# Two declared orders in a two-layer decoder kernel: the second half of w_out behind the projection's last copies, the head outputs behind the gates' sixth product

## The chip, the core and the metric

The kernel runs on one core of a Trainium2 chip. The core has TensorE (PE, matrix products; "PEld" is its loading of weights), VectorE (DVE), ScalarE (ACT), GpSimd (POOL) and SyncE (SP, which here only starts transfers). Each engine works through its own list of instructions in order and waits, at the instruction whose turn it is, for semaphores of the others. The metric is the device time of one execution in microseconds (us).

## What is computed

Two layers of a decoder trunk on a sequence of 512 tokens with 1024 channels, all in float32. The part of a layer that the change touches is the end of the mixer:

```python
y_b = (jax.nn.silu(g_r) * y_r.reshape(B, S, RET_V_WIDTH)).astype(x.dtype)
merged = (jax.nn.sigmoid(gate_a) * jnp.einsum('bsc,cd->bsd', y_a, w_attn_proj)
          + jax.nn.sigmoid(gate_b) * jnp.einsum('bsc,cd->bsd', y_b, w_ret_proj))
return jnp.einsum('bsd,de->bse', merged, w_out)
```

`gate_a` and `gate_b` are columns of the input projection `x @ w_in + b_in`; `y_r` is the output of the four retention heads (2048 wide), `y_a` that of the attention (384 wide). Behind it come a residual with layer norm, a SwiGLU feed-forward part of width 2816, and a second layer norm.

## The kernel before, in words

Every float32 product is made of three faster ones. A value is split into a high part (a cast on ACT to the format that PE reads fast) and a low part (value minus high, on DVE), and PE adds high x high, high x low and low x high. The helper `hilo` (L106) does one split: one ACT instruction and one DVE instruction. Weights are loaded into buffers called `raw` (eight of 128 x 1024), split into `whi` and `wlo` (four each) and used. SP issues most loads in its own order; each waits until the buffer that it fills is free. POOL issues those that add to a buffer (L348, L1162), and also the transfers of the residual (L1349) and of the norm's parameters (L1360); the first step of the layer norm's root (L147) runs on POOL too.

Large products are cut into two by two blocks and computed with seven block products instead of eight (the Strassen-Winograd scheme). They are numbered 1 to 7 and run in the order 1, 2, 5, 3, 6, 7, 4 (`ORDER`). Some share an accumulator in PSUM (`CHAIN`): 1, 6, 7 and 4 add up in the two banks "A", 5 and 3 in "C". Between two products of one chain the sum so far has to be copied out (`sn`) before PE may go on adding to that bank.

The places that matter, in the order of the program in each layer:

- **The gates.** `gates(0)` and `gates(1)` (L1117) run such a scheme through `biased` (L501). Its `ev` is called behind each product for each half `a`: products 1, 5 and 6 are copied on ACT (L510, kept in the list `evicted`); product 2 is added in `left` (L1123); the result of product 3 is combined on DVE (L514) when product 6 is done; product 7 is subtracted on DVE (L517). The sigmoids of the right half are written to DRAM (`g_d`, L1132).
- **The head outputs.** During `gates(1)` the retention outputs are read back from DRAM (`y_d`) into `yr` (L1111). They are split into the left operand of the next product: `y_put` (L1113) writes quarters of `xh` and `xl`, and `s1` (L1164) forms one difference and splits it into `xs`. Three little instructions (L1145 to L1148) exist only to give this work a dependence on the gates: two casts write one or two columns of `xh` from a gate tile, and `one` is a scalar 1.0 computed from that tile, by which `s1` multiplies.
- **The attention weights** (`was`): eight small sums of nine matmuls, each multiplied into a gate tile `sg` on DVE (L1241).
- **The projection** with w_ret_proj, 28 weight units in the seven products, four units each. Unit n+2 is split while unit n is used (`emit`). Copies (`copies`, L1285), sums (L1327 to L1333) and gating (`gated`: L1268, L1269) follow the products, and the gated rows are transposed by PE (L1276) and split into `m`.
- **The output projection** with `m` and w_out: units 28 to 31 are the first half of w_out's columns, `stream[28:]`; the second half, `wo[4:]`, is split into the free `xs` by `tail_units` (L307). Results go to the residual `xtok` (L1379), the layer norm follows, and `xtok` is transposed (L205).

A scheduling framework sets the order of the instructions on each engine from dependences and its own estimate of times; where nothing binds two instructions, that estimate decides. `behind` (L83) declares an order of two instructions on one engine, without a semaphore. `seq` (L86) does so for a running chain per engine: while `chain` holds an entry for the engine, each instruction given to `seq` is put behind the one before it. The projection switches this on with `chain.update(act=None, dve=None)` and off with `chain.clear()`.

Of the kernel before, what the change touches and what calls it, by code (L numbers as in the profile page):

```python
# [12 lines left out]
F32 = mybir.dt.float32  # L13
# [3 lines left out]
ALU = mybir.AluOpType  # L17
# [3 lines left out]
P = 128  # L21
# [35 lines left out]
def hybrid_kernel(ctx, tc, x, rel_bias, w_in, b_in, w_attn_proj, w_ret_proj, w_out,  # L57
# [3 lines left out]
    pe, act, dve, pool = nc.tensor, nc.scalar, nc.vector, nc.gpsimd  # L61
# [4 lines left out]
    sm = ctx.enter_context(tc.tile_pool(name="sm", bufs=4, side="right"))  # L66
# [9 lines left out]
    xh = keep.tile([P, KD, S], F32R, name="xh")  # L76
    xl = keep.tile([P, KD, S], F32R, name="xl")
    xs = keep.tile([P, 4, 2, 4, 256], F32R, name="xs")
    dve.memset(mhalf, -0.5)

    evicted, chain = [], {}

    def behind(inst, other):  # L83
        tc.add_manual_dep(inst.ins, other.ins.name, ORDERED, reason="order on one engine")

    def seq(engine, inst):  # L86
        if engine in chain:
            if chain[engine] is not None:
                behind(inst, chain[engine])
            chain[engine] = inst  # L90
# [13 lines left out]
        return psm.tile([P, S], F32, tag="mm", name=name)  # L104

    def hilo(src, hi, lo):  # L106
        seq("act", act.copy(out=hi, in_=src))  # L107
        seq("dve", dve.tensor_tensor(out=lo, in0=src, in1=hi.bitcast(F32), op=ALU.subtract))  # L108

    def raw(name="raw"):  # L110
        return rawp.tile([P, 1024], F32, tag="raw", name=name)
# [1 line left out]
    def work(name):  # L113
        return wk.tile([P, S], F32, tag="w2", name=name)
# [194 lines left out]
    def tail_units(raws):  # L309

        out_ = []
        for j, r in enumerate(raws):
            v = xs[:, j].rearrange("p h k t -> p h (k t)").rearrange("p h (a b) -> p h a b", a=2)
            hilo(r, v[:, 0], v[:, 1])
            out_.append((v[:, 0], v[:, 1]))
        return out_
# [94 lines left out]
    def tall(right, n, left, ev, bias_=None):  # L411


        ps = {}
        for (i, an, bn), units in zip(ORDER, right.operands()):
            ks = [(u, k) for u in units for k in range(u[0].shape[1])]
            c = CHAIN[i]
            for a in range(2):
                fresh = i in FIRST
                if fresh:  # L420
                    ps[c, a] = psum("ps")[:, :n]
                if bias_ is not None and i in (1, 5):
                    o = (i != 1) * RV
                    mm(ps[c, a], pick[:, bias_:bias_ + 1].to_broadcast([P, P]), bh[:, o:o + n], True, False)
                    fresh = False
                ts_ = slice(a * P, (a + 1) * P)
                for j, ((h, l), k) in enumerate(ks):
                    p_ = ps[c, a]
                    ah, al = left(an, j, ts_)
                    mm(p_, ah, h[:, k], fresh and j == 0, False)  # L430
                    mm(p_, ah, l[:, k], False, False)
                    mm(p_, al, h[:, k], False, j == len(ks) - 1)
                    tick(STEP * n / 512)
                if i != 3:
                    ev(i, a, ps[c, a])
                if i == 6:
                    ev(3, a, ps["C", a])
            yield
# [63 lines left out]
    def biased(right, n, row, left, right_done):  # L502


        sn = {}

        def ev(i, a, ps):
            if i in (1, 5, 6):
                sn[i, a] = work("sn")[:, :n]
                evicted.append(act.copy(out=sn[i, a], in_=ps))  # L510
            elif i == 2:
                left(a, ps, sn[1, a])
            elif i == 3:
                dve.tensor_tensor(out=sn[6, a], in0=ps, in1=sn[6, a], op=ALU.subtract)  # L514
                right_done(a, sn[6, a])
            elif i == 7:
                dve.tensor_tensor(out=sn[5, a], in0=sn[5, a], in1=ps, op=ALU.subtract)  # L517
                right_done(2 + a, sn[5, a])
            elif i == 4:
                left(2 + a, ps, None)  # L520

        return tall(right, n, x_left, ev, row)
# [175 lines left out]
    def layer(ly, cp):  # L698
# [81 lines left out]
        with stage("attn") as ap_, stage("attw", 4) as aw:  # L780
# [62 lines left out]
            if ly == 0:  # L843
# [20 lines left out]
                for hf in range(2):  # L864
                    for i in range(2):
                        load_x(i, hf)
                    for g, j in tiles:
                        c = (C_QA, C_KA)[j] + g * GW
# [10 lines left out]
                late = []  # L879
# [95 lines left out]
            bias, tail = {}, []  # L975
            load_bias(0)
            for hp in range(HPG // 2):
# [21 lines left out]
                tail = t_  # L999
# [10 lines left out]
        with ret:  # L1010
# [81 lines left out]
            sga, ya, yb = [None] * NI, [], [[None, None], [None, None]]  # L1092
# [10 lines left out]
            def y_blocks():  # L1103
                yas.close()
                ret.close()
                sbp[0] = lay.enter_context(stage("sbp"))
                yr = yrs.enter_context(stage("yr", side="right"))
                for a, b in ((0, 0), (1, 0), (1, 1), (0, 1)):
                    yb[a][b] = [yr.tile([P, 4, 256], F32, tag=f"yr{a}{b}{u}", name="yr") for u in range(2)]
                    for u in range(2):  # L1110
                        nc.sync.dma_start(yb[a][b][u], y_part(a, b, u))  # L1111

            def y_put(o, u, r):  # L1113
                ks, ts_ = slice(4 * u, 4 * u + 4), slice(o, o + 256)
                hilo(r, xh[:, ks, ts_], xl[:, ks, ts_])

            def gates(c):  # L1117

# [19 lines left out]
            for n_, _ in enumerate(gates(1)):  # L1138
                if n_ == 0:
# [1 line left out]
                    for t in range(NG):  # L1141
                        ya_put(t)
                    y_blocks()
            late = sga[1][:, 1]
            act.copy(out=xh[:, 0:8:4, 0:1], in_=late[:, 0:2].unsqueeze(2))  # L1145
            act.copy(out=xh[:, 0, 256:257], in_=late[:, 0:1])
            one = sm.tile([P, 1], F32, tag="one", name="one", bufs=1)
            dve.tensor_scalar(one, late[:, 0:1], 0.0, 1.0, op0=ALU.mult, op1=ALU.add)  # L1148

            def block_w(b, u):  # L1150
                k = 8 * (b[1] == "2") + 2 * u
                c = (b[2] == "2") * S
                return wr_l[:, k:k + 2, c:c + S]
# [8 lines left out]
                pool.dma_start(r, block_w(b, u), accum_op=ALU.add)  # L1162

            def s1(u):  # L1164
                dve.scalar_tensor_tensor(out=a22[u], in0=a21[u], scalar=one, in1=a22[u], op0=ALU.mult, op1=ALU.subtract)
                hilo(a22[u], xs[:, u, 0], xs[:, u, 1])

            def s3_raw(u):
# [29 lines left out]
                o = 256 * (an[1] == "2" or an == "A12") + ts_.start  # L1198
                return xh[:, j, o:o + P], xl[:, j, o:o + P]

            for u in range(2):
                y_put(0, u, a11[u])
            for u in range(2):
                y_put(256, u, a12[u])
            for u in range(2):
                s1(u)
            more = [lambda f=f, u=u: f(u) for f in (s3_raw, s2_raw, s2_put, s4_raw, s4_put, s3_put) for u in range(2)]
# [2 lines left out]
            b22, wo, stream = [], [], []  # L1210

            def emit(n):
                g, u = divmod(n, 4)
                if g in (0, 2, 4, 6):
                    stream.append(unit(pch[u]))
                    if g in (0, 4):
                        add(pch[u], ("B12", "", "B21")[g // 2], u)
                elif g == 1:
                    stream.append(unit(b21[u]))
                    b22.append(load(block_w("B22", u), 2, S))  # L1220
                elif g in (3, 5):
                    stream.append(unit(b22[u]))
                    if g == 3:
                        seq("dve", dve.tensor_tensor(out=pch[u], in0=pch[u], in1=b22[u], op=ALU.add))
                        add(b22[u], "B12", u)
                else:
                    stream.append(unit(wo[u]))
                if g in (5, 6):
                    wo.append(load(wo_l[:, 2 * u:2 * u + 2, (g - 5) * S:(g - 4) * S], 2, S))

            for hf in range(2):
                for i in range(NI):
                    ps = psum("ps")
                    ks = [(u, k) for u in was[hf] for k in range(u[0].shape[1])]
# [53 lines left out]
            pss, sn = {}, {}  # L1288
            chain.update(act=None, dve=None)
            for n in range(28):  # L1290
                g, u = divmod(n, 4)
                i, an, _ = ORDER[g]
                c = CHAIN[i]
# [31 lines left out]
                for a in range(2):  # L1325
# [9 lines left out]
                    elif i == 4:  # L1335
                        if a == 0:
                            drain()
                        gated(2 + a, 0, pss[c][a], o_=work("sn"))
            chain.clear()
            emit(30)  # L1340
            emit(31)
        lay.close()

        fin = ExitStack()
# [40 lines left out]
        with stage("lp") as lp:  # L1385
            xc = [[lp.tile([P, 4, 256], F32, name=f"xc{a}{b}") for b in range(2)] for a in range(2)]
            ln_par(lp.tile([P, 2 * D], F32, name="lnp"), ln1_g[ly], ln1_b[ly])

            def m_tok(k, i):
                return (m[k // 4][:, e, k % 4, i * P:(i + 1) * P] for e in range(2))  # L1390

            def evo(hf, i, ps):
                residual(i, hf, ps, True, True)
                if hf == 1:
                    norm(i)
                    side.extend([nothing] * (6, 2, 5, 4)[i] + to_xT(xtok(i), i, xc))

            units = [stream[28:], tail_units(wo[4:])]
            for hf, toks in ((0, (0, 1)), (1, (0,)), (1, (1,)), (0, (2, 3)), (1, (2,)), (1, (3,))):
                while any(turns[i] for i in toks):  # L1400
                    side.popleft()()
                xstat(units[hf], S, m_tok, lambda i, ps, hf=hf: evo(hf, i, ps), toks=toks)
# [113 lines left out]
        for part, (f0, f1) in enumerate(FPARTS):  # L1516
# [31 lines left out]
            units = [[unit(r) for r in raws[0]], tail_units(raws[1])]  # L1548
# [67 lines left out]
```

## Time and profile before

| what | value |
| --- | --- |
| device time, median of 3 runs | 2111.55 us (2108.3 to 2112.28) |
| profiled execution, its time | 2108.74 us |
| its span in the trace | 2107.0 us |
| instructions | 33728 |
| busy: PE, weight loads, DVE, ACT, POOL | 99%, 88%, 79%, 54%, 13% |
| granted TensorE clock | 0.999 |
| moved by DMA | 366 MB, 174 GB/s over the span |

How to read the rows: an instruction row of the timeline has its start and its length in us from the span's start, the engine, the line of the kernel, the operation, "out<-in" by the program's names and the shapes, and in brackets how long the engine sat idle before it and what ended that. Ends of matmuls are modelled and overlap, so the step from one start to the next tells more than the length. A row of waits has the waiting engine, operand and line, what it waited for, and then the total in us, how many times, and the longest. "PE ps L96" are the matmuls of all products, since one helper records them.

### The profile page before, as it was taken

The page shows a single profiled execution, that of the slowest core. Times are in us where ns is not written, and L with a number is a line of the kernel's source. Part 1 is how long each engine was busy: PE and PEld are TensorE (multiplying, and loading weights), DVE is VectorE, ACT ScalarE, POOL GpSimd, SP SyncE. Part 2 cuts the span into 40 slices and gives each one's busy share as a digit, 9 for nine tenths or more (in the row PEclk, how much of TensorE's full clock was granted, in tenths as well). Part 3 has the DMA queues.
Part 4 walks back from the last instruction along what each step waited for, and adds up shares of the span by engine and source line. Part 5 has one row for each costly group of instructions (what it writes and reads, how often), then busy time and mean ns, then how long its engine had stood idle before and what let it go on. Part 6 is the DMA issues. An engine that isn't in the chain of part 4 may idle for free.

```text
span 2107.0 us, 33728 instructions
## 1 busy us (share of the span) xinstructions
PE 2079.4 (99%) x13130; PEld 1852.7 (88%) x13130; DVE 1656.0 (79%) x2359; ACT 1144.4 (54%) x1751; POOL 279.8 (13%) x280
## 2 busy tenths in 40 slices
PE   9999999999999999999999999999999999999998
PEld 8989888888787898999899898888887879989897
DVE  7666888786886698887787578897868877988876
ACT  5567654655654365555355766555655534655551
POOL 3111111101021101111030111111000211110101
PEclk9999999999999999999999999999999999999999
DMA  8866557666968358868258554657668782687771
GB/s 244 209 175 140 134 142 193 171 165 168 290 158 261 81 146 209 192 155 229 81 154 232 135 139 129 179 148 206 174 167 268 168 262 64 175 194 178 194 192 46
DMA packets 303297, 365.99 MB, mean 174 GB/s; under 512 B 22685, under 2 KB 214329, under 8 KB 303008
## 3 DMA queue, kind: packets, MB, share of 16 engines
q1 hardware_dynamic: 211904, 250.91, 37.6%
q0 software_dynamic: 63824, 100.11, 26.1%
q10 hardware_dynamic: 27408, 12.80, 2.2%
q8 instruction: 103, 1.69, 0.3%
q14 instruction: 58, 0.48, 0.1%
HBM read 342.11 MB, written 24.33 MB: 174 GB/s over the span
## 4 chain that ended last, share of the span: by engine, by line
PE 82%; DMA 6%; DVE 5%; issue 5%; ACT 1%; POOL 0%; POOLq 0%; DVEq 0%; SPq 0%; ACTq 0%
PE ps L96 73%; PE px L96 6%; DMA y_d<-yt 3%; DVE wlo L365 1%; DMA raw<-in_w_in 1%; PE px L596 1%; DMA yr<-y_d 1%; DVE wlo L108 1%; PE px L1058 1%; PE px L205 1%; DVE xs L108 1%; DMA raw<-in_w_out 1%; ACT whi L357 0%; DVE gb L1268 0%; POOL ry L147 0%
## 5 line engine op out<-in xcount | busy, mean ns | idle before, releaser
L365 DVE TENSOR_TENSOR wlo<-raw,whi 128x1024 fp32r<-128x1024 f32 (+1 forms) x518 | 602.3, 1172 | 175.9 <-ACT whi L357 162.1
L357 ACT CAST whi<-raw 128x1024 fp32r<-128x1024 f32 (+1 forms) x518 | 516.1, 1008 | 388.9 <-PE ps L96 145.0
L96 PE MATMUL ps<-xs,whi 128*128 128x256 f32 x2176 | 399.5, 284 | 0.4 <-ACT sn L828 0.4
L96 PE MATMUL ps<-whi,xs 128*128 128x512 f32 (+1 forms) x1152 | 349.2, 373 | 3.4 <-ACT sn L510 2.3
L96 PEld LDWEIGHTS ps<-xs,whi 128*128 128x128 f32 x2176 | 339.4, 192 | 4.9 <-issue 1.7
L96 PE MATMUL ps<-xh,whi 128*128 128x256 f32 (+1 forms) x1104 | 318.3, 290 | 1.7 <-ACT xh L107 1.4
L96 PE MATMUL ps<-xl,whi 128*128 128x256 f32 (+1 forms) x1104 | 315.5, 286 | 0.0
L96 PE MATMUL ps<-xh,wlo 128*128 128x256 f32 (+1 forms) x1104 | 315.0, 286 | 0.0
L96 PE MATMUL ps<-xs,wlo 128*128 128x256 f32 x1088 | 308.0, 283 | 1.2 <-DVE wlo L365 1.2
L96 PEld LDWEIGHTS ps<-whi,xs 128*128 128x128 f32 x1152 | 210.0, 188 | 40.0 <-ACT sn L510 4.0
L96 PEld LDWEIGHTS ps<-xh,whi 128*128 128x128 f32 x1104 | 210.3, 191 | 9.7 <-ACT xh L107 2.8
L96 PEld LDWEIGHTS ps<-xl,whi 128*128 128x128 f32 x1104 | 211.4, 191 | 3.0 <-DVE xl L108 0.6
L96 PE MATMUL ps<-wlo,xs 128*128 128x512 f32 (+1 forms) x576 | 213.2, 370 | 0.8 <-DVE wlo L365 0.8
L96 PEld LDWEIGHTS ps<-xh,wlo 128*128 128x128 f32 x1104 | 211.2, 191 | 1.5
L96 PEld LDWEIGHTS ps<-xs,wlo 128*128 128x128 f32 x1088 | 208.5, 192 | 1.8 <-DVE wlo L365 1.8
L96 PE MATMUL ps<-whi,xh 128*128 128x512 f32 (+1 forms) x512 | 193.7, 378 | 7.7 <-ACT sn L1285 5.3
L348 POOL DMA_DIRECT2D raw<-in_w_in x80 | 97.2, 1224 | 712.6 <-DMA raw<-in_w_in 235.5
L96 PE MATMUL ps<-wlo,xh 128*128 128x512 f32 (+1 forms) x512 | 190.8, 373 | 0.0
L96 PE MATMUL ps<-whi,xl 128*128 128x512 f32 (+1 forms) x512 | 190.2, 372 | 0.0
L381 DVE TENSOR_TENSOR raw<-raw 128x1024 f32<-128x1024 f32 (+1 forms) x148 | 171.8, 1168 | 0.8
L96 PE MATMUL ps<-whi,ht 128*128 128x512 f32 x544 | 170.1, 391 | 0.0
L107 ACT CAST whi<-raw 128x1024 fp32r<-128x1024 f32 (+1 forms) x102 | 100.6, 1001 | 97.3 <-PE ps L96 78.6
(247 smaller groups left out, 3272.8 us busy)
## 6 DMA issues: line engine op xcount, KB each, us to landing
raw<-in_w_in SPq DMA_DIRECT2D x168, 512.0 KB, 5.1
raw<-in_w_in POOLq DMA_DIRECT2D x64, 512.0 KB, 8.4
raw<-in_w_ffn_up SPq DMA_DIRECT2D x64, 512.0 KB, 4.6
raw<-in_w_ffn_down SPq DMA_DIRECT2D x52, 512.0 KB, 4.8
raw<-in_w_ffn_gate SPq DMA_DIRECT2D x44, 512.0 KB, 5.2
raw<-in_w_ffn_gate POOLq DMA_DIRECT2D x40, 512.0 KB, 7.1
raw<-in_w_in SPq DMA_DIRECT2D x56, 256.0 KB, 4.7
raw<-in_w_ret_proj SPq DMA_DIRECT2D x24, 512.0 KB, 4.4
```

Source lines behind the costliest of these rows:

```text
L96: pe.matmul(ps, lhsT=a, rhs=b, start=start, stop=stop, skip_group_check=True)
L107: seq("act", act.copy(out=hi, in_=src))
L108: seq("dve", dve.tensor_tensor(out=lo, in0=src, in1=hi.bitcast(F32), op=ALU.subtract))
L205: pe.transpose(px[:, d * P:(d + 1) * P], src[:, (4 * hf + d) * P:(4 * hf + d + 1) * P], ident)
L348: pool.dma_start(r, self.src({"P1": "B12", "P3": "B22"}[n], u), accum_op=ALU.add)
L357: c = act.copy(out=h, in_=src)
L365: dve.tensor_tensor(out=l, in0=src, in1=h.bitcast(F32), op=ALU.subtract)
L381: dve.tensor_tensor(out=r, in0=r, in1=self.t["B22" if n == "P2" else "B21", u], op=ALU.add)
L596: pe.transpose(px[:, hh, j * P:(j + 1) * P], ss[od][:, hh, j * P:(j + 1) * P], ident)
L1058: pe.transpose(px[:, t * P:(t + 1) * P], ys[i][:, t * P:(t + 1) * P], ident)
```

## The change

It does three things, all of them to orders.

First, `ev` keeps the DVE instruction that combines product 3 (in the new list `combined`). The head outputs' work no longer has its artificial dependence: the two casts, the scalar `one` and the multiplication by it are removed. Instead each of the four `y_put` casts is declared to stand behind the last copy of the gates (`evicted[-1]`), and each `s1` behind the last combination (`combined[-1]`); `s1` is a plain subtraction.

Second, `tail_units(wo[4:])` is called before `chain.clear()` and not after it, so its four splits stand in the chain behind everything that went through `seq` before: on ACT behind the last casts of weight units 30 and 31, on DVE behind the last gating and those units' low parts.

Third, `hilo` and `y_put` return their two instructions, so that they can be named.

```diff
-    evicted, chain = [], {}
+    evicted, combined, chain = [], [], {}
...
     def hilo(src, hi, lo):
-        seq("act", act.copy(out=hi, in_=src))
-        seq("dve", dve.tensor_tensor(out=lo, in0=src, in1=hi.bitcast(F32), op=ALU.subtract))
+        c = act.copy(out=hi, in_=src)
+        d = dve.tensor_tensor(out=lo, in0=src, in1=hi.bitcast(F32), op=ALU.subtract)
+        seq("act", c)
+        seq("dve", d)
+        return c, d
...
             elif i == 3:
-                dve.tensor_tensor(out=sn[6, a], in0=ps, in1=sn[6, a], op=ALU.subtract)
+                combined.append(dve.tensor_tensor(out=sn[6, a], in0=ps, in1=sn[6, a], op=ALU.subtract))
                 right_done(a, sn[6, a])
...
             def y_put(o, u, r):
                 ks, ts_ = slice(4 * u, 4 * u + 4), slice(o, o + 256)
-                hilo(r, xh[:, ks, ts_], xl[:, ks, ts_])
+                return hilo(r, xh[:, ks, ts_], xl[:, ks, ts_])
...
-            late = sga[1][:, 1]
-            act.copy(out=xh[:, 0:8:4, 0:1], in_=late[:, 0:2].unsqueeze(2))
-            act.copy(out=xh[:, 0, 256:257], in_=late[:, 0:1])
-            one = sm.tile([P, 1], F32, tag="one", name="one", bufs=1)
-            dve.tensor_scalar(one, late[:, 0:1], 0.0, 1.0, op0=ALU.mult, op1=ALU.add)
-
...
             def s1(u):
-                dve.scalar_tensor_tensor(out=a22[u], in0=a21[u], scalar=one, in1=a22[u], op0=ALU.mult, op1=ALU.subtract)
+                behind(dve.tensor_tensor(out=a22[u], in0=a21[u], in1=a22[u], op=ALU.subtract), combined[-1])
                 hilo(a22[u], xs[:, u, 0], xs[:, u, 1])
...
-            for u in range(2):
-                y_put(0, u, a11[u])
-            for u in range(2):
-                y_put(256, u, a12[u])
+            for o, r in ((0, a11), (256, a12)):
+                for u in range(2):
+                    behind(y_put(o, u, r[u])[0], evicted[-1])
...
-            chain.clear()
             emit(30)
             emit(31)
+            tail = tail_units(wo[4:])
+            chain.clear()
         lay.close()
...
-            units = [stream[28:], tail_units(wo[4:])]
+            units = [stream[28:], tail]
```

What the order of the instructions becomes, in layer 0 (layer 1 is the same). New lines are three higher than old ones up to L1146 and three or four lower behind.

ACT in `gates(1)`, from the last sigmoid of product 2 on, before. `xh<-yr` are head casts, `sn<-ps` the copies of product 5, `whi` casts of the gates' weights:

```order
L1126 ACTIVATE sg_5386<-sn_5716 128x512
L1145 CAST xh_79<-sg_5386 128x2
L1146 CAST xh_79<-sg_5386 128x1
L107 CAST xh_79<-yr_5735 128x4x256
L107 CAST xh_79<-yr_5736 128x4x256
L510 COPY sn_5811<-ps_5797 128x512
L510 COPY sn_5827<-ps_5813 128x512
L357 CAST whi_5833<-raw_5656 128x1024
```

and now:

```order
L1129 ACTIVATE sg_5386<-sn_5716 128x512
L513 COPY sn_5811<-ps_5797 128x512
L513 COPY sn_5827<-ps_5813 128x512
L360 CAST whi_5833<-raw_5656 128x1024
L360 CAST whi_5836<-raw_5659 128x1024
L360 CAST whi_5865<-raw_5662 128x1024
L360 CAST whi_5868<-raw_5665 128x1024
L513 COPY sn_5883<-ps_5686 128x512
```

The head casts have left the place between the gate and the copies of product 5; the first of them now stands behind both copies of product 6 and the two weight casts that follow.

DVE in `gates(1)` before, from the first head difference to the second subtraction of product 7 (`sn<-ps,sn` are L514, `sn<-sn,ps` L517):

```order
L1165 SCALAR_TENSOR_TENSOR yr_5743<-yr_5739,one_5979,yr_5743 128x1024
L365 TENSOR_TENSOR wlo_5834<-raw_5656,whi_5833 128x1024
L365 TENSOR_TENSOR wlo_5837<-raw_5659,whi_5836 128x1024
L381 TENSOR_TENSOR raw_5656<-raw_5656,raw_5652 128x1024
L381 TENSOR_TENSOR raw_5659<-raw_5659,raw_5654 128x1024
L365 TENSOR_TENSOR wlo_5866<-raw_5662,whi_5865 128x1024
L365 TENSOR_TENSOR wlo_5869<-raw_5665,whi_5868 128x1024
L108 TENSOR_TENSOR xl_80<-yr_5747,xh_79 128x4x256
L514 TENSOR_TENSOR sn_5883<-ps_5797,sn_5883 128x512
L108 TENSOR_TENSOR xs_81<-yr_5743,xs_81 128x1024
L1165 SCALAR_TENSOR_TENSOR yr_5744<-yr_5740,one_5979,yr_5744 128x1024
L514 TENSOR_TENSOR sn_5901<-ps_5813,sn_5901 128x512
```

and now, from the second weight operation behind the same point on:

```order
L368 TENSOR_TENSOR wlo_5869<-raw_5665,whi_5868 128x1024
L517 TENSOR_TENSOR sn_5883<-ps_5797,sn_5883 128x512
L517 TENSOR_TENSOR sn_5901<-ps_5813,sn_5901 128x512
L1162 TENSOR_TENSOR yr_5743<-yr_5739,yr_5743 128x1024
L368 TENSOR_TENSOR wlo_5912<-raw_5656,whi_5911 128x1024
L520 TENSOR_TENSOR sn_5811<-sn_5811,ps_5686 128x512
L368 TENSOR_TENSOR wlo_5915<-raw_5659,whi_5914 128x1024
L108 TENSOR_TENSOR xl_80<-yr_5735,xh_79 128x4x256
L520 TENSOR_TENSOR sn_5827<-sn_5827,ps_5702 128x512
```

The two differences and the head operations have moved from in front of the two combinations to behind them.

ACT at the end of the projection before, from the cast of weight unit 25 on (`m1<-px` follow PE's transposes, `sn<-ps` are the copies of product 7, `xs<-raw` the second half of w_out):

```order
L107 CAST whi_6636<-raw_6007 128x1024
L107 CAST xs_81<-raw_6615 128x1024
L107 CAST m1_6409<-px_6654 128x4x128
L1285 COPY sn_6661<-ps_6142 128x512
L1285 COPY sn_6662<-ps_6143 128x512
L107 CAST whi_6671<-raw_6009 128x1024
L107 CAST whi_6689<-raw_6011 128x1024
L107 CAST xs_81<-raw_6640 128x1024
```

and now:

```order
L107 CAST whi_6632<-raw_6003 128x1024
L107 CAST m1_6405<-px_6650 128x4x128
L1281 COPY sn_6657<-ps_6138 128x512
L1281 COPY sn_6658<-ps_6139 128x512
L107 CAST whi_6667<-raw_6005 128x1024
L107 CAST whi_6685<-raw_6007 128x1024
L107 CAST whi_6703<-raw_6525 128x1024
```

The four `xs` casts, and their four low parts on DVE, now follow the split of unit 31. On PE the transposes of the gated rows in product 4 (L1276, now L1272) stand five and sixteen matmuls later than before, and in layer 0 the first transposes of `xtok` (L205, now L208) two matmuls earlier. On SP two loads of `gb` change places with one of w_ret_proj; the list of POOL is the same.

## The prediction, as made before the changed kernel was run

> **What bounds the kernel now.** I read the page's head first, then who TensorE (PE) waited for, then the timelines of the stretches that the change touches, with PE's rows beside those of ScalarE (ACT) and VectorE (DVE).
>
> ```profile
> span 2107.0 us, 33728 instructions
> PE 2079.4 (99%) x13130; PEld 1852.7 (88%) x13130; DVE 1656.0 (79%) x2359; ACT 1144.4 (54%) x1751; POOL 279.8 (13%) x280
> ...
> PE ps L96 <- ACT sn L1285: 5.5, 3, 2.8
> PE ps L96 <- ACT sn L510: 2.3, 3, 1.3
> PE ps L96 <- DVE sn L517: 1.8, 4, 0.6
> PE px L1276 <- DVE sg L1269: 1.1, 2, 0.5
> ```
>
> PE is the bound: of 2107 us it is idle for 2107.0 - 2079.4 = 27.6. No faster engine can give more, and a change of order alone can only give back waits. The four rows (total, times, longest) are 10.7 us of it, and most of that lies in the two stretches that this change reorders, once in each layer. So every removed wait counts fully, and anything moved into PE's way costs fully.
>
> The second gates call, layer 0. The products run in the order 1, 2, 5, 3, 6, 7, 4; each is two halves of 12 matmuls.
>
> ```profile
> 542.87 1.05 ACT L107 CAST xh<-yr 128x1024 fp32r<-128x1024 f32 x1 [0.73 <-DMA yr<-y_d]
> 544.61 1.05 ACT L107 CAST xh<-yr 128x1024 fp32r<-128x1024 f32 x1 [0.69 <-DMA yr<-y_d]
> 545.56 1.07 ACT L510 COPY sn<-ps 128x512 f32<-128x512 f32 x2
> ...
> 544.52 0.39 PE L96 MATMUL ps<-whi,xs 128*128 128x512 f32 x1
> 546.19 0.50 PE L96 MATMUL ps<-whi,xs 128*128 128x512 f32 x1 [1.29 <-ACT sn L510]
> ...
> 549.30 1.28 DVE L1165 SCALAR_TENSOR_TENSOR yr<-yr,one 128x1024 f32<-128x1024 f32 x1 [2.39 <-DMA yr<-y_d]
> 558.45 0.68 DVE L514 TENSOR_TENSOR sn<-ps,sn 128x512 f32<-128x512 f32 x1
> 559.17 0.64 ACT L1131 ACTIVATE sb<-sn 128x512 f32<-128x512 f32 x1 [3.59 <-DVE sn L514]
> 560.33 0.50 PE L96 MATMUL ps<-whi,xs 128*128 128x512 f32 x1 [0.22 <-ACT sn L510]
> 563.12 0.68 DVE L517 TENSOR_TENSOR sn<-sn,ps 128x512 f32<-128x512 f32 x1
> 563.95 0.47 PE L96 MATMUL ps<-whi,xh 128*128 128x512 f32 x1 [0.58 <-DVE sn L517]
> ...
> 1591.80 0.50 PE L96 MATMUL ps<-whi,xs 128*128 128x512 f32 x1 [0.83 <-ACT sn L510]
> 1609.26 0.47 PE L96 MATMUL ps<-whi,xh 128*128 128x512 f32 x1 [0.60 <-DVE sn L517]
> ```
>
> Product 3 accumulates into the banks of product 5, so it needs product 5's copies (`sn`, L510). Those stand on ACT behind two head casts that wait for transfers: PE loses 1.29. DVE then waits at L1165 for another transfer, 2.39, with six weight operations behind it; so the gates' sums (L514, L517) come late and PE loses 0.22 and 0.58. The last two rows are the same places in layer 1.
>
> The end of the projection, both layers:
>
> ```profile
> 653.24 0.60 PE L1276 MATMUL px<-ident,sg 128*128 128x128 f32 x4
> 654.54 1.04 ACT L107 CAST xs<-raw 128x1024 fp32r<-128x1024 f32 x1 [2.35 <-DMA raw<-in_w_out]
> 655.49 0.58 ACT L107 CAST m<-px 128x512 fp32r<-128x512 f32 x1
> 655.97 1.08 ACT L1285 COPY sn<-ps 128x512 f32<-128x512 f32 x2
> 656.61 0.50 PE L96 MATMUL ps<-whi,xh 128*128 128x512 f32 x1 [2.78 <-ACT sn L1285]
> ...
> 660.02 1.22 DVE L108 TENSOR_TENSOR xs<-raw,xs 128x1024 fp32r<-128x1024 f32 x1
> 662.96 0.69 DVE L1269 TENSOR_TENSOR sg<-sg,gb 128x512 f32<-128x512 f32 x1
> 663.56 3.49 DVE L108 TENSOR_TENSOR wlo<-raw,whi 128x1024 fp32r<-128x1024 f32 x3
> 663.79 0.63 PE L1276 MATMUL px<-ident,sg 128*128 128x128 f32 x4 [0.54 <-DVE sg L1269]
> ...
> 1698.16 0.60 PE L1276 MATMUL px<-ident,sg 128*128 128x128 f32 x4
> 1700.62 1.08 ACT L1285 COPY sn<-ps 128x512 f32<-128x512 f32 x2
> 1701.26 0.50 PE L96 MATMUL ps<-whi,xh 128*128 128x512 f32 x1 [2.50 <-ACT sn L1285]
> 1708.44 0.63 PE L1276 MATMUL px<-ident,sg 128*128 128x128 f32 x4 [0.55 <-DVE sg L1269]
> ```
>
> Here product 4 needs product 7's copies (L1285). They stand behind one cast of the second w_out weights (`xs`), which waits 2.35 for its load.
>
> **The change, part by part.** Times are on the clock of before; a shift that both sides share is left out.
>
> Gates. The casts and the L1165 operation now stand behind the copies, so nothing ahead of them waits for y_d. Product 5 ends at 544.75: copy, then the four weight casts (1.0 each) while product 3 runs, DVE's part right behind. Product 3 and product 6's first half take 36 matmuls of about 0.23 (the 48 of the `xs` row quoted below last 692.72 - 681.52 = 11.2 us), so product 6's first copy falls near 553.0 and L514 near 553.8 instead of 558.45; the second pair near 556.3. One moved subtraction (1.22) and one weight operation (1.22) later, L517 ends near 560.0; PE, no longer delayed, wants it at 561.1. Its second half ends near 562.9 for a need at 563.8, with one more weight operation and one head operation ahead. So all three waits go: 1.29 + 0.22 + 0.58 = 2.09 in layer 0, 0.83 + 0.60 = 1.43 in layer 1: **3.52**. The cover is thin there, 0.9 to 1.1 us; without it the 0.6 us waits come back.
>
> What they are moved past: head casts that stood inside the gates now run at the start of the products with the attention weights, and four of the DVE halves, 1.2 us each, stand ahead of the multiplications by L1241. These start near 574.5, six us after their first bank is full. A bank fills every 9 x 0.23 = 2.1 us, so four are full by then; there are eight, so PE does not notice. If it did, each bank short would cost 0.6, one such multiplication. The two tiny casts, the scalar and the multiply by one (L1165: 1.28 against the 1.22 of a plain subtraction) save 0.5 us a layer off the path: nothing.
>
> Projection. With the `xs` cast gone, the cast of `m` follows its transposes, at 653.24 + 0.60 + 0.03 = 653.87 instead of 655.49, and the copies at 654.35 instead of 655.97: 1.62 earlier. The `m` cast stays ahead of the copies, so about 1.2 of the wait remains. Layer 1 likewise: 1698.16 + 1.11 = 1699.27 for 1700.62, 1.35. Together **2.97**.
>
> Behind it DVE drops three `xs` operations, and the transposes of L1276 now stand five and more matmuls later on PE: `sg` ends near 659.2 and is wanted near 662. The waits 0.54 + 0.55 = **1.09** go. Next late is the third product-4 weight (first of the three `wlo` at 663.56): DVE ends it near 660.4, PE wants it near 660.7; if late, a few tenths.
>
> A wait costs more than its bracket: 544.52 to 546.19 is 1.67, less a pitch of 0.23 is 1.44, 0.15 above the bracket. For the seven waits that vanish, 7 x 0.15 = **1.05**.
>
> The four moved pairs (ACT 1.06, DVE 1.22 each) now follow the last copies: DVE reaches them near 670.7 and ends them near 675.3, PE wants the first near 679:
>
> ```profile
> 681.52 11.36 PE L96 MATMUL ps<-xs,m 128*128 128x512 f32 x48
> 698.32 0.63 PE L205 MATMUL px<-ident,xtok 128*128 128x128 f32 x4 [0.29 <-issue]
> ...
> 691.05 1.29 POOL L348 DMA_DIRECT2D raw<-in_w_ffn_gate  x1 [13.49 <-DMA raw<-in_w_ffn_gate]
> 691.93 1.10 POOL L147 TENSOR_TENSOR ry<-ve,mhalf 128x1 f32<-128x1 f32 x1
> ...
> 692.92 0.69 DVE L1379 SCALAR_TENSOR_TENSOR xtok<-xtok,ps 128x512 f32<-128x512 f32 x1 [2.56 <-PE ps L96]
> ...
> 664.00:668.00 4.00, 4.00 (x20) 3.08 (x19) 4.00 (x5) 2.54 (x4) 0.00 (x0) 1.00 0.78 238
> 684.00:688.00 4.00, 4.00 (x19) 3.22 (x18) 0.71 (x2) 0.00 (x0) 0.00 (x0) 1.00 1.10 250
> ...
> DMA to landing us min/median/max: 3.1/5.4/15.2
> ```
>
> (The two rows of stretches give length, then busy us of PE, weight loads, DVE, ACT and POOL, granted clock, DMA share, GB/s; the last row is for the weight buffers `raw` from 600 to 700.)
>
> The 679 is 681.52 less the 2.4 gained in the projection. Three us and more of slack: cost nothing; without it PE would pay every us that the first pair is late. In layer 0 the transposes of `xtok` also move two matmuls forward on PE, into a wait that DVE sets: minus 0.3.
>
> Sum: 3.52 + 2.97 + 1.09 + 1.05 - 0.3 = **8.3 us**. The profiled execution took 2108.74; less 8.3 it is 2100.4. The median of the runs shown is 2108.3 to 2112.28 about 2111.55, 2.8 above it, and on that scale I forecast 2103.2.
>
> One cost the trace does not show: what SP's and POOL's queues do when four weight loads keep their buffers longer. SP's loads of the feed-forward weights wait for those buffers and POOL's L348 for the loads; L147, the root that the layer norm needs, stands behind L348 on POOL. From below it is a gain: the residual's two transfers on POOL wait for the last gate operations, which now run 3 us earlier against PE, so the crowded stretch (the 684:688 row, DMA share 1.10) ends up to 3 us sooner. From above, L348 comes as much later as the buffers do, 2.4 us against PE. L147 ends at 693.0, and in the new order DVE uses it behind the next token's sum and statistics, 692.92 + 2 x 0.7 = 694.3; 1.3 of the 2.4 are covered, PE waits at L205 for 1.1 a layer. I take nothing, for the same bytes move and start earlier.
>
> [...]
>
> **The rivals.**
> *Only the gates part pays* (16%). The wait behind the `m` cast stays, and the saved 1.6 comes back at the next weight: wlo is 0.3 us from being late. Then the gain is 3.52 + 0.75 (five waits) = 4.3, time 2107.3. For it: DVE is full (4.00 of 4.00 us in the 664:668 row). Against: it loses three `xs` operations of 1.22 there.
> *Everything goes* (8%). The remaining 1.2 to 1.4 per layer vanish as well, if the cast of `m` starts before the last transpose has ended: 8.3 + 2.7 = 11, time 2100.5. Against: it reads what all four write.
> *The order does not decide* (8%): the gates' waits are replaced by equal ones on `wlo` or behind the moved subtraction, and the projection gives half; a gain near 2, time 2109.5. For it: the covers of 0.9 to 1.1. Against: the transfer that L1165 waited for is there by 549.3 and is wanted only near 557.
> *Slower* (4%): POOL's queue. If the load that L348 waits for lands later still, L147 and with it L205 slip one for one. It must slip (8.3 + 4.2) / 2 = 6.3 us in each layer beyond the 1.3 to eat the gain and 4.2 more, time 2116. For it: a landing took up to 15.2 us here, and L348 waited 13.49. Against: the residual's transfers, which crowd it, start earlier.
>
> **How the numbers follow.** 64% for 8.3 as worked out, its own range 2100 to 2106 (the thin covers of 0.3 to 1.1 us, twice, and the scatter of the median). About 0.2%, 4.2 us, is what a measurement of this kernel can tell from no change. Faster by more: 64 + 8 + half of the gates-only case = 80%; within: 8 + 8 = 16%; slower: 4%. The range reaches to the gates-only case and a little past it, and down to everything gone with a low median: 2098 to 2109.
>
> **What would show it.** Right: no wait for `sn` L513 or L520 (now the lines of L510, L517) in the second gates call, a remaining wait for L1281's copies of 1.1 to 1.5 us in each layer, none for `sg` at L1272, none for `xs`. Wrong: a new wait on `wlo` L108 in product 4, on `xs` in the output projection, or more than 1 us at the first `xtok` transposes.

## The result, and the profile after

The changed kernel takes 2100.47 us (median of 6 runs, 2097.18 to 2104.76) for 2111.91 before (6 runs, 2108.3 to 2113.13): a ratio of 0.9948, 95% interval 0.9934 to 0.9962. It is 11.4 us faster; 8.3 had been forecast. A second set of 5 runs, below, gave 2099.34 and 0.9942 (0.9928 to 0.9955).

The head of the page of the changed kernel, and from its list of PE's waits the rows that belong to the reordered stretches (total, times, longest):

```profile
span 2095.4 us, 33729 instructions
PE 2075.1 (99%) x13130; PEld 1853.3 (88%) x13130; DVE 1654.6 (79%) x2357; ACT 1143.3 (55%) x1747; POOL 279.3 (13%) x280
...
PE ps L96 <- ACT sn L1281: 3.4, 4, 1.2
PE px L208 <- issue: 1.0, 1, 1.0
```

From these stretches the waits for the gates' copies and subtractions and the one for `sg` are gone; the one for the projection's copies (L1281, before L1285) fell from 2.8 to 1.2 at its longest; the wait of 1.0 at the first transposes of `xtok` was 0.29 before.

The second gates call, layer 0, in the timeline of the changed kernel:

```profile
552.82 0.69 DVE L517 TENSOR_TENSOR sn<-ps,sn 128x512 f32<-128x512 f32 x1 [0.31 <-ACT sn L513]
558.41 0.68 DVE L520 TENSOR_TENSOR sn<-sn,ps 128x512 f32<-128x512 f32 x1
560.15 0.39 PE L96 MATMUL ps<-whi,xh 128*128 128x512 f32 x1
561.28 0.68 DVE L520 TENSOR_TENSOR sn<-sn,ps 128x512 f32<-128x512 f32 x1
562.88 0.39 PE L96 MATMUL ps<-whi,xh 128*128 128x512 f32 x1
```

The combination L517 starts at 552.82 and not at 558.45. The two subtractions end at 559.09 and 561.96; PE takes up the banks at 560.15 and 562.88 without a bracket, 1.06 and 0.92 us later.

The end of the projection, layer 0, and the first use of the moved splits:

```profile
649.80 0.60 PE L1272 MATMUL px<-ident,sg 128*128 128x128 f32 x4
650.43 0.58 ACT L107 CAST m<-px 128x512 fp32r<-128x512 f32 x1 [1.67 <-PE px L1272]
650.91 1.08 ACT L1281 COPY sn<-ps 128x512 f32<-128x512 f32 x2
651.56 0.50 PE L96 MATMUL ps<-whi,xh 128*128 128x512 f32 x1 [1.17 <-ACT sn L1281]
655.16 0.69 DVE L1265 TENSOR_TENSOR sg<-sg,gb 128x512 f32<-128x512 f32 x1
658.50 0.60 PE L1272 MATMUL px<-ident,sg 128*128 128x128 f32 x4
668.48 4.62 DVE L108 TENSOR_TENSOR xs<-raw,xs 128x1024 fp32r<-128x1024 f32 x4
L96 PE MATMUL ps<-xs,m x19: 392/394/399, 675.6 to 679.8; 128*128 128x512 f32 x19
```

The cast of `m` follows its transposes, the copies follow the cast, and 1.17 us remain. `sg` is ready at 655.85 for transposes at 658.50. The moved splits end at 673.10, 2.5 us before PE's first use at 675.6 (the last row is of the view by tile, with first and last start).

What is new: POOL's queue ahead of the first layer norm.

```profile
683.10 0.15 DVE L149 TENSOR_SCALAR ve<-mv 128x1 f32<-128x1 f32 x1
684.29 1.31 POOL L351 DMA_DIRECT2D raw<-in_w_ffn_gate  x1 [16.23 <-DMA raw<-in_w_ffn_up]
686.98 1.29 POOL L351 DMA_DIRECT2D raw<-in_w_ffn_gate  x1 [1.38 <-DMA raw<-in_w_ffn_gate]
687.86 1.11 POOL L150 TENSOR_TENSOR ry<-ve,mhalf 128x1 f32<-128x1 f32 x1
691.30 1.28 DVE L1369 SCALAR_TENSOR_TENSOR xtok<-xtok,ry,lnp 128x1024 f32<-128x1024 f32 x1
692.68 0.63 PE L208 MATMUL px<-ident,xtok 128*128 128x128 f32 x4 [1.05 <-issue]
```

Both adding loads wait for a feed-forward load that comes later than before, against PE. SP's rows for the loads of the `up` weights ahead of them, before and now:

```profile
665.94 5.57 SPq L125 DMA_DIRECT2D raw<-in_w_ffn_up  x4
667.46 8.20 SPq L128 DMA_DIRECT2D raw<-in_w_ffn_up  x4
```

PE's first product with `xs` starts at 681.52 before and at 675.6 now, so these loads start 15.6 us ahead of it before and 8.1 us now. The root L150, whose input is there at 683.25, stands behind them until 687.86; the last multiplication starts at 691.30, and PE loses 1.05.

Where the time went, by the time between the starts of the same matmuls (PE's 13130 matmuls keep their number; each column cuts them at the same counts; us; the repeated runs are those of the next section):

| stretch (clock of the first profile of before) | before, four profiles | changed, two | gates part alone | projection part alone |
| --- | --- | --- | --- | --- |
| gates, layer 0 (540 to 575) | 34.89, 35.21, 35.25, 34.94 | 31.75, 31.75 | 31.75 | 35.91 |
| gates, layer 1 (1586 to 1620) | 33.97, 31.75, 34.41, 33.65 | 31.75, 31.75 | 31.75 | 34.63 |
| end of projection, layer 0 (640 to 676) | 35.96, 37.59, 37.58, 38.04 | 33.45, 33.49 | 37.52 | 33.46 |
| end of projection, layer 1 (1690 to 1722) | 31.82, 31.58, 32.79, 32.83 | 29.61, 29.65 | 31.69 | 29.62 |
| first `xtok` transposes, layer 0 (690 to 705) | 15.07, 15.09, 15.08, 15.07 | 15.87, 15.74 | 15.11 | 15.65 |

By the means of the rows the change gives 3.32 + 1.70 + 3.82 + 2.63 - 0.73 = 10.7 us. The first profile of before, on which the prediction was built, gives only 3.14 + 2.22 + 2.51 + 2.21 - 0.80 = 9.3: it was a good execution of that kernel, and the experiments say why. One row varies most: in layer 1 the gates lose nothing (31.75) in the second profile of before, whose PE had lost 2.69 us just ahead of them, and 1.90 to 2.66 in the others.

### The profile page after: what moved, and what is told of

Read it like the earlier page. It is cut to its first block, busy times and chain, and to the rows that moved or that the text cites. A ratio compares the mean times of both kernels' runs of the same rounds, so it can differ in the third digit from the quotient of the medians.

```text
span 2095.4 us, 33729 instructions
## 1 busy us (share of the span) xinstructions
PE 2075.1 (99%) x13130; PEld 1853.3 (88%) x13130; DVE 1654.6 (79%) x2357; ACT 1143.3 (55%) x1747; POOL 279.3 (13%) x280
## 4 chain that ended last, share of the span: by engine, by line
PE 88%; issue 4%; DVE 3%; DMA 2%; ACT 1%; POOL 0%; SPq 0%; POOLq 0%; DVEq 0%; ACTq 0%
PE ps L96 79%; PE px L96 6%; DMA raw<-in_w_in 1%; PE px L599 1%; DVE wlo L368 1%; PE px L1061 1%; DVE wlo L108 0%; DMA y_d<-yt 0%; PE px L208 0%; DMA yr<-y_d 0%; PE px L1272 0%; POOL ry L150 0%; ACT whi L360 0%; DVE raw L380 0%; DVE xs L108 0%
```

## The experiments

**Before and changed, again.** No edit. Between the two first profiles 11.6 us of span had gone. A list of long steps, on which the first expectation rests, puts 4.3 of them outside the reordered stretches; by the table it is 11.6 - 9.3 = 2.3.

> The kernel before, unchanged, for a second profile and the scatter. Between the two profiles at hand 11.6 us of span went; the stretches that the change reorders account for some 7.3 of it (steps from one matmul's start to the next, less the usual step), and the other 4.3 lie elsewhere, most of it in four places: 331.5 (0.53), 404.2 (0.20), 1133.6 with 1134.8 (1.66) and 1574.3 (0.82). Theory 'scatter': these come and go between executions, so that this second profile lacks at least half of the 3.2 us there and its PE waits in the reordered places are the same as before (1.4, 0.4, 0.75, 2.9, 0.8 in layer 0). Theory 'caused by the order': they are all here again within 0.3 us. Time 2111.9 by both, ratio 1.000 within 0.001.

> The changed kernel, unchanged. Time 2100.5, ratio 0.9948 (0.9934 to 0.9962). Theory 'scatter': its profile shows one or two of the stalls at about 331, 404, 1128 and 1569 again, and the wait at the first transposes of the residual tokens (1.2 us in the first profile) may be another number. Theory 'caused by the order': none of these stalls, a span within 1 us of 2095.4. Both: the wait behind product 7's copies is 1.3 us in each layer again.

Measured: 2112.54 (ratio 1.0003, 0.9993 to 1.0013) and 2099.34. Of the four places named, the second profile of before lacks 404 and most of 1134 (0.17 for 1.66), but at 332 it has 0.92 and at 1576 it lost 2.85; the second profile of the changed kernel has 0.49, 0.63 and three of 0.34 to 0.47 at those three places. Neither theory holds as it was put: the second profile of before loses 0.92 + 0.17 + 2.85 = 3.9 us at the four places, not under 1.6, and not the same as the first within 0.3 at each. The stalls come and go, and no gain is read from them. But this second profile of before was 3.7 us longer than the first, and part of that lies in the reordered stretch itself: behind the wait in front of product 4 eight matmuls took 0.427 us each and not 0.227.

**One part at a time.**

The gates part alone is the changed kernel with

```diff
-            emit(30)
-            emit(31)
-            tail = tail_units(wo[4:])
             chain.clear()
+            emit(30)
+            emit(31)
...
-            units = [stream[28:], tail]
+            units = [stream[28:], tail_units(wo[4:])]
```

and the projection part alone is the kernel before with the same lines the other way round.

> Head outputs and their differences behind the gates' copies and combinations as in the change; the second half of w_out as before, outside the chain. Theory 'the waits add up': gain 3.52 + 5 x 0.15 = 4.3 us, ratio 0.9980; the waits at product 7's copies stay at 2.5 to 2.9 us in each layer. Rival 'pinned to the load': the cast of w_out waits for a load that does not come sooner when PE does, so the 2.1 (layer 0) and 1.4 (layer 1) gained in the gates come back there: those waits grow to 4 to 5 us and the gain is under 1.5 us, ratio over 0.9993.

> The second half of w_out inside the chain as in the change; the head outputs as before, with the two small casts, the scalar and the multiplication. Theory 'the waits add up': gain 2.97 + 1.09 + 2 x 0.15 - 0.3 = 4.1 us, ratio 0.9981; the gates' waits 1.45, 0.38, 0.75 in layer 0 and 0.99, 0.76 in layer 1 stay, product 7's wait falls to 1.3 in each layer. Rival 'pinned to the load': the whole gain of the change, 8 us or more, ratio 0.9962 or less, since the gates' gain only came through by this part.

Measured: gates alone 2105.42, ratio 0.9973 (0.9964 to 0.9982); projection alone 2106.58, 0.9972 (0.9960 to 0.9983). The two parts add up: 0.27 and 0.28% for 0.52 and 0.58% together. With the gates alone the longest wait for the copies is still 2.8:

```profile
PE ps L96 <- ACT sn L1281: 6.3, 4, 2.8
```

The rival that the wait is pinned to the load wanted 4 to 5 there; it falls. Each part gave more than its 4.1 to 4.3 us, though the intervals hold these. The table shows that the projection part alone brings the new cost at `xtok` (15.65), the gates part none (15.11).

**Before, twice more.** No edit.

> The kernel before once more, for a third profile. Theory 'the clock takes part of the difference': the wait of 2.9 to 3.2 us in front of product 4 in layer 0 is followed by eight matmuls at 0.427 us in some executions and not in others (none in the first profile, eight in the second); where they show, the execution is 1.6 us longer for each such place. Rival: the second profile was an exception, and neither this one nor the next shows any.

> The kernel before, for a fourth profile, with the same two expectations as for the third: slowed matmuls behind the wait in front of product 4 in some executions, or in none but the second.

The third profile of before shows the slowed matmuls in layer 0 and in layer 1, and so does the fourth (2112.32 and 2112.99 us, spans 2110.5 and 2111.2), so the second was no exception. The third, PE's rows in layer 0, and the view by stretches (length, then PE, weight loads, DVE, ACT, POOL busy, granted clock, DMA share, GB/s):

```profile
653.24 0.60 PE L1276 MATMUL px<-ident,sg 128*128 128x128 f32 x4
656.77 0.50 PE L96 MATMUL ps<-whi,xh 128*128 128x512 f32 x1 [2.93 <-ACT sn L1285]
657.42 0.63 PE L96 MATMUL ps<-whi,xl 128*128 128x512 f32 x1
657.84 0.63 PE L96 MATMUL ps<-whi,xh 128*128 128x512 f32 x1
...
656.70:657.40 0.70, 0.63 (x2) 0.50 (x3) 0.70 (x2) 0.70 (x3) 0.00 (x0) 0.89 0.00 0
657.40:660.40 3.00, 3.00 (x8) 2.31 (x7) 2.93 (x6) 2.64 (x3) 0.00 (x0) 0.50 0.55 175
660.40:663.00 2.60, 2.60 (x12) 2.19 (x11) 1.59 (x2) 1.58 (x2) 0.00 (x0) 0.95 0.16 18
```

The granted clock is 0.50 for 3 us behind the wait. Eight matmuls lose 8 x (0.427 - 0.227) = 1.6 us in such a stretch. By the table one costs less, 1.4 to 1.5 us in layer 0 and 1.1 in layer 1, when the step in front of it is taken off on both sides: the wait for `sg` behind it, 0.54 and 0.55 in the first profile, is then 0.4 in layer 0 and gone in layer 1. At this place the four profiles of before have 0, 1, 2 and 2 of them, the two of the changed kernel none. The lists of runs, which give a mean granted clock for every execution, say the same: 0.9973 on average over 58 executions of before, 0.9988 over 11 of the changed kernel. A stretch of 3.4 us at half speed lowers the mean over 2100 us by 0.0008, so the difference is about two stretches. Not all of them lie behind the wait that the change shortens: of the six in the four profiles five do, and one stands behind another wait, at 1576. Of the 58 executions only 6 have the 0.999 of the profile that the prediction was made from; they took 2109.9 on average, the 28 with 0.997 took 2113.0.

**The wait made longer on purpose**, in the changed kernel; `extra` is 2 or 4 for product 7, else 0.

```diff
-                for t, ps in zip(ts, pss):
-                    seq("act", act.copy(out=t, in_=ps))
+                for t, ps, again in zip(ts, pss, (extra, 0)):
+                    for _ in range(1 + again):
+                        seq("act", act.copy(out=t, in_=ps))
```

> The changed kernel, with the copy of product 7's first bank made three times and not once: 2 x 0.49 us more of ACT in front of product 4, in each layer, nothing else moved. The step from the transposes to product 4's first matmul grows from 1.44 to 2.4 us. Both theories (a wait costs its length; a wait over about 3.07 us also slows TensorE's clock behind it): plus 2 x 0.97 = 1.9 us, 2102.0, no slowed matmuls behind the wait.

> The same with five copies of that bank: 4 x 0.49 us more in each layer, a step of 3.4 us. Theory 'a wait costs its length': plus 2 x 1.95 = 3.9 us on the changed kernel, 2104.0, the matmuls behind the wait at 0.227 us each. Theory 'clock': in the second profile of before and in the one with the gates alone, steps of 3.08, 3.12 and 3.22 us were each followed, about a microsecond behind them, by eight matmuls at 0.427 us (granted clock 0.50 to 0.53 over 3.4 us), steps of 3.05 and less by none; so here both layers show eight such matmuls, 8 x 0.2 = 1.6 us each: plus 3.9 + 3.2 = 7.1 us, 2107.2.

Measured: 2105.03, ratio 0.9968 (0.9956 to 0.9979), and 2108.75, 0.9987 (0.9977 to 0.9997). A repeated copy took 0.62, not 0.49, so the steps became 2.67 and 3.91 us. With four extra copies both layers slow down (the stretches behind the wait in layers 0 and 1):

```profile
656.40:659.80 3.40, 3.40 (x10) 2.67 (x9) 3.30 (x6) 1.24 (x3) 0.00 (x0) 0.52 0.00 0
...
1701.10:1704.40 3.30, 3.30 (x9) 2.55 (x8) 3.23 (x5) 1.25 (x2) 0.08 (x1) 0.50 0.00 0
```

By length alone the time would be 2099.3 + 2 x (3.91 - 1.44) = 2104.2; with two slow stretches of 1.6 us 2107.4. The second is what was measured, within the scatter. With two extra copies both theories had expected no slowing, and both were wrong:

```profile
652.64 0.50 PE L96 MATMUL ps<-whi,xh 128*128 128x512 f32 x1 [2.40 <-ACT sn L1282]
1695.42 0.50 PE L96 MATMUL ps<-whi,xh 128*128 128x512 f32 x1 [2.40 <-ACT sn L1282]
...
650.00:652.60 2.60, 0.24 (x3) 0.00 (x0) 0.69 (x1) 2.26 (x5) 0.00 (x0) 1.00 0.57 204
652.60:653.20 0.60, 0.56 (x2) 0.52 (x3) 0.58 (x1) 0.60 (x2) 0.00 (x0) 0.90 0.12 41
653.20:656.20 3.00, 3.00 (x8) 2.34 (x7) 2.86 (x6) 1.76 (x2) 0.00 (x0) 0.50 0.00 0
1692.80:1695.40 2.60, 0.22 (x3) 0.00 (x0) 0.69 (x1) 2.28 (x5) 0.00 (x0) 1.00 0.63 199
1695.40:1696.40 1.00, 0.98 (x4) 0.85 (x5) 0.96 (x2) 1.00 (x2) 0.00 (x0) 1.00 0.03 8
1696.40:1699.40 3.00, 3.00 (x14) 2.45 (x14) 2.90 (x5) 2.26 (x3) 0.00 (x0) 1.00 0.00 0
```

The same wait of 2.40 us slowed layer 0 and not layer 1: behind it the granted clock is 0.50 over 3 us in the one (8 matmuls) and 1.00 in the other (14). So 3.07 is no threshold, and the length of a wait alone does not decide; what else does is not shown.

**The copies ahead of the last cast of `m`.**

```diff
-                        gated(a, 1, sn[6][a], 5)
+                        gated(a, 1, sn[6][a], 6)
...
-                        gated(2 + a, 1, sn[5][a])
+                        gated(2 + a, 1, sn[5][a], 3)
```

> The changed kernel with the transposes of product 6's gated rows one place later in PE's side list (5 to 6) and those of product 7 one earlier (4 to 3), so that on ACT product 7's copies stand ahead of the last cast of m and not behind it. Theory 'the copies stand behind the cast': the bank of the first half is full six matmuls (1.4 us) before the product ends, its copy is done by then, and the step of 1.44 us in each layer falls to 0.1 to 0.3; gain 2 x 1.2 = 2.4 us on the changed kernel, 2097.5, ratio to before 0.9931. Rival 'the next weight is late' (the covers of 0.3 us): the wait comes back on the low part of product 4's first weights, gain under 0.8 us, ratio over 0.9938.

```profile
649.16 0.59 ACT L1281 COPY sn<-ps 128x512 f32<-128x512 f32 x1
650.07 0.59 ACT L1281 COPY sn<-ps 128x512 f32<-128x512 f32 x1 [0.31 <-PE ps L96]
651.94 0.59 ACT L107 CAST m<-px 128x512 fp32r<-128x512 f32 x1 [0.33 <-PE px L1272]
```

The first copy now runs while product 7's second half is still going on, and PE shows no wait there in either layer: the stretch is 32.08 and 28.23 us for 33.45 and 29.61, 1.4 less each. The time, 2097.84 and a ratio of 0.9936 (0.9922 to 0.9950), lies the right way but is not told apart from the changed kernel's by its interval; the trace is what shows it.

**The root ahead of the adding loads.** `roots` is a list of the roots, L150.

```diff
-                        pool.dma_start(r, self.src({"P1": "B12", "P3": "B22"}[n], u), accum_op=ALU.add)
+                        d = pool.dma_start(r, self.src({"P1": "B12", "P3": "B22"}[n], u), accum_op=ALU.add)
+                        if len(roots) in (4, 12):
+                            behind(d, roots[-4])
```

> The changed kernel with one order more: in POOL's list the two adding loads of the feed-forward weights stand behind the root of the first token tile of the layer norm, not ahead of it. Theory 'POOL's queue': the root runs at about 683.3 and not at 687.9, and PE's step of 1.2 to 1.4 us at the first transposes of the residual tokens in layer 0 (0.69 in the kernel before) falls to 0.3 or less; gain 1.0 us, 2099.0. Rival: the step is set by DVE, which only gets to the last multiplication at 691.3 behind the second tile's statistics; the step stays over 0.9 us and the time at 2100.

```profile
684.62 1.54 POOL L150 TENSOR_TENSOR ry<-ve,mhalf 128x1 f32<-128x1 f32 x1 [15.27 <-DVE ve L149]
686.12 1.35 POOL L351 DMA_DIRECT2D raw<-in_w_ffn_gate  x1
...
692.29 0.60 PE L208 MATMUL px<-ident,xtok 128*128 128x128 f32 x4
```

The root waits for its own input only, PE does not wait at all, and the stretch at `xtok` is 14.62 us for 15.87. That settles POOL's queue as the cause. The time was 2097.81 (0.9931, 0.9918 to 0.9945); by its interval alone it is not told apart from the changed kernel's.

**All three orders.** As well as the last two, in the projection the head operation of unit 11 moves behind product 5's copies.

```diff
-                if more:
+                if more and n != 11:
                     more.pop(0)()
...
                     sn[i] = copies(pss[c])
+                if n == 11:
+                    more.pop(0)()
```

> The changed kernel with three more orders: product 7's copies ahead of the cast of m, the roots ahead of the adding loads, and in the projection the last head cast (which waits for a reload of head outputs) behind product 5's copies and not ahead of them. Theory 'the waits add up': 2.4 (copies) + 1.1 (root) + the steps of 0.5 to 1.0 us behind the transposes before product 3 in each layer, 1.2 together: 4.7 us under the changed kernel's 2100, so 2095.2, ratio to before 0.992. Rival 'the next one is late': a wait for a weight's low part or for the cast takes their place, time 2097.5, no better than either order alone.

Measured: 2094.06 (2093.45 to 2094.76), ratio 0.9908 (0.9891 to 0.9924). Its interval lies clear under both of the changed kernel's (0.9934 to 0.9962, 0.9928 to 0.9955). The copies stand ahead of the head cast that waits for its reload, and no bracket is left in front of product 3:

```profile
615.48 0.59 ACT L1283 COPY sn<-ps 128x512 f32<-128x512 f32 x1 [0.77 <-PE ps L96]
615.96 1.05 ACT L107 CAST xh<-yr 128x1024 fp32r<-128x1024 f32 x1
617.00 0.48 PE L96 MATMUL ps<-whi,xs 128*128 128x512 f32 x1
```

This version beats both kernels, and the waits added up as expected (2095.2).

## Why the prediction was right, and where it was off

Time and sign: 2100.47 lies in the range of 2098 to 2109, nearer to its lower end than to the forecast of 2103.2. The gain was forecast too small, 8.3 for 11.4. That the median meets the 2100.4 worked out from the profiled execution is chance: the profiled execution of the changed kernel took 2097.18.

- **Gates, 3.52.** Right in mechanism and in its clock: the ends of the subtractions were worked out with covers of 1.1 and 0.9 us and measured with 1.06 and 0.92. All five waits that were named are gone. The size in layer 1 was that of one execution: 1.43 had been set, and the four profiles of before lose 2.22, 0.00, 2.66 and 1.90 there.
- **A wait costs 0.15 more than its bracket.** Mis-sized. The matmul behind a wait is late as well: 546.19 to the next start was 0.34, not 0.23. So it is 0.15 + 0.11, about 0.25, and smaller steps follow: the gates' stretches gave 3.14 + 2.22 = 5.36 against the same first profile for 3.52 + 5 x 0.15 = 4.27.
- **Projection, 2.97 + 1.09.** Right: the remaining wait is 1.17 where 1.2 had been left, the cast starts with its transposes' end (649.80 + 0.60 + 0.03 = 650.43), `sg` and `xs` are in time (slack 2.5 us where over 3 was worked out). Against the first profile the stretches gave 2.51 + 2.21 = 4.72 for 4.36.
- **The profiled execution stands for the kernel.** This is the step that failed. The prediction took the 2.8 us between that execution and the median as a scale to be carried over. In part they were slow stretches behind the wait that the change shortens: the clock of before is 0.9973 on average, 0.999 in that execution. The change removes these too, 1.1 to 1.5 us wherever one occurred, 5 in the four profiles. The three other profiles of before are 3.9 us longer than the first on average; 1.9 of it lies in the five stretches of the table, the other 1.9 elsewhere, most of it at 1576 in one of them. So about half of the scale was something that the change takes away, and the forecast carried all of it over.
- **SP's and POOL's queues, taken as nothing.** Wrong, though bounded: from above 1.1 a layer had been worked out, and it cost 0.73 in layer 0, where 0.3 had been set for the moved transposes, and nothing at this place in layer 1. The reason given for nothing, that the same bytes start earlier, does not hold: against PE the loads of the `up` weights start 7.4 us later (15.6 - 8.1), where 2.4 had been set as the most. The mechanism of the last rival is there, in small. What decided was the order in POOL's own list, as the run with the root ahead shows; there the stretch is 14.62, so the moved transposes themselves cost nothing.
- **The rivals.** "Only the gates part pays" falls by the run with the projection part alone. "Everything goes" names the right time, 2100.5, for a wrong reason: the wait behind the cast of `m` stayed. "The order does not decide" falls with the table's 31.75, the same in every run with the new order. "Slower" named the queue that does cost something, but far from the 6.3 us a layer that it needed.

The sum afterwards: from the first profile gates 5.36, projection 4.72, `xtok` -0.80, makes 9.3; by the means of the table, which hold the slow stretches, 10.7. The medians differ by 11.4 in the first set of runs and by 12.6 in the second (2111.98 - 2099.34). What is left lies elsewhere (1075 to 1200 and 1560 to 1586 above all), where single executions of one kernel differ by more than that; no run shows that the order causes it.

## What to carry to other kernels

Look at the granted clock of several executions before taking one profile as the base: the one at hand can be an execution in which a long wait happened not to slow the clock. In the four profiles of before PE's waits for the projection's last copies (2.78 and 2.50 us in the first) cost 1.1 to 1.5 us beyond their length five times out of eight, and nothing more than it the other three. And where an order puts buffers free later, follow the loads into every queue that waits for them, down to the small instruction that stands behind: here a root of 1.1 us.

## What the runs showed of the hardware

**The clock after a wait.** In the profiles of this case 16 steps of PE from one matmul to the next lie between 2.5 and 4 us. Behind ten of them some eight matmuls ran at 0.427 us and not at 0.227, beginning up to 1.6 us behind the wait, with a granted clock of 0.50 to 0.53 over some 3.4 us: 3.71, 3.22, 3.20, 3.08, 2.66 and 2.62 in the second to fourth profile of before, 3.12 with the gates part alone, 3.91 twice with four extra copies, 2.67 in layer 0 with two. Behind six none did: 3.05 and 2.77 in the first profile of before, 2.67 in layer 1 with two extra copies, and 2.66, 2.61 and 2.52. In these runs, then, the length of the step alone does not tell whether the clock falls: 3.05 did not slow it and 2.62 did, and one of two equal steps of 2.67. What else decides is not shown.

**A transfer's issue on ACT took up to 4.72 us.** In the second profile of before the store of a retention output held ACT's list for 4.72 us, in the first of the changed kernel the one at the same place 1.03:

```profile
1572.95 4.72 ACTq L1061 DMA_DIRECT2D y_d<-yt  x1
1577.72 0.60 ACT L1126 ACTIVATE sg<-ps 128x512 f32<-128x512 f32 x1 [3.85 <-issue]
1579.30 0.50 PE L96 MATMUL ps<-whi,xh 128*128 128x512 f32 x1 [2.69 <-ACT whi L357]
```

The weight casts behind it came late, and PE lost 2.69 us and a slow stretch. In the first profile of before the same issue took 2.67 us, and PE waited 0.66 us for a weight cast: in both, PE's wait is 2.0 us shorter than the issue. The DMA share was 1.1 there in the second profile. PE's loss there is 0.82 us in the first and 2.85 in the second; why the issue takes so long is open.
